# Keeping split weight parts in DRAM, lending idle PSUM banks and re-ordering a written-out instruction list in a one-core transformer layer

## The chip, the cores and the metric

The kernel runs on one core of a Trainium2 chip. The metric is the device time of one execution in microseconds (us). Five engines work side by side, each through its own instruction stream in order: TensorE (PE, matmuls), VectorE (DVE), ScalarE (ACT), GpSimd (POOL) and SyncE (SP, which here only issues DMAs). POOL also issues DMAs, through a queue of its own.

## The reference

One decoder layer on 1024 tokens of width 1024: a half-step SwiGLU FFN, a mixing stage of two attentions side by side, and a second half-step FFN. The change lies in the mixing stage:

```python
merged = jax.nn.sigmoid(gate_a) * (y_a @ w_o_a[l]) + jax.nn.sigmoid(gate_b) * (y_b @ w_o_b[l])
x = x + merged @ w_out[l]
```

`gate_a` and `gate_b` are columns of one projection of the normed input, `y_a` is a sparse attention over the 256 best keys of each token, `y_b` a stick-breaking attention. `w_o_a` and `w_o_b` are 512 x 1024, `w_out` is 1024 x 1024, all in float32.

## The kernel before, in words

**Matrix products.** Every float32 operand is split in a high part (rounded to the PE's float32r by an ACT copy) and a low part (the rest, a subtraction on POOL or DVE), and each product is three matmuls: high x high, high x low, low x high (`mm3`, L310 to L314). A weight that is read raw from DRAM so costs an ACT copy and a POOL subtraction (`split`, L293; in the mixing stage `weights`, L1107).

**The order of the program.** First FFN, then the mixing stage, then the second FFN. In the mixing stage the order on PE, DVE, ACT and POOL is written out by a planner that runs when the program is built. Each piece of work is a Python generator that yields what it needs next; `Weave.run` steps the one that can start first by a table of durations (`Weave.cost`, L113), with ranks as tie-breaks. What it emits is the order that the chip then follows; the order is fixed, the waits are semaphores. Outside the mixing stage the tile framework's own scheduler orders the instructions, and it orders the SP stream everywhere.

**PSUM.** In the mixing stage there are eight banks of 128 x 512 float32: two `fbank` (projections: `psf` for gates, `psuv`, `psob`, `psoa`), three `ubank` (`psdot`, `psz`, later the logits `psL`), two `vbank` (transposes) and one `wbank` (`psy`, `pso`). A gate projection (`fproj`, L1196, called in `fillers`, L1285) is 24 matmuls in one `fbank`; ACT reads it out (`gate_out`, L1226) into a ring of three small tiles `evr`, and POOL stores it in DRAM (`gd`).

**The end of the mixing stage.** `project` (L2199) multiplies by `w_o_b` for both token halves (`psob`, stored as `obd`) and by `w_o_a` for the first half (`psoa`, stored as `md`); sets `oa0`, `oa2`, `oa4`, `oa6` are 256 columns each, as high and low tiles of 512 KB in a ring of four (two sets). The other half's `y_a` is ready last. So `w_o_a` is read and split again for it: `woa0`, `woa2` in the planned part, `woa4`, `woa6` behind it. There (L2247 on) `psm` are 8 x 12 matmuls; a tile `gate` takes `gd` and `obd` (two loads of 256 KB each), DVE multiplies and adds, and the result `m` is split (`M0`).

**w_out.** A second `project` (L2281) multiplies by `w_out` for one half, then for the other. Each half takes eight sets of `w_out` (`wout{half}{n}{j}`, 512 KB raw), 24 matmuls `psout` each. Raw tiles come from a ring of four, split parts from `op`, a ring of nine. The set for the second half is the same weight as for the first, read and split again. `x2d` stores the new residual; `b0r`, `b1r` are raw weights of the second FFN.

**A shared port.** The planner's table holds that POOL and DVE instructions with long operands in SBUF slow each other (`shared` in `flush`).

## Time and profile before

| | us |
|---|---|
| median of three runs (lowest, highest) | 2126.56 (2125.76, 2130.45) |
| the profiled execution | 2126.26 |
| its span, from the first to the last instruction | 2124.5 |
| PE busy in the span | 2100.6 |
| POOL, ACT, DVE busy | 913.5, 1063.6, 1521.6 |

A row of the timeline gives the start, the duration, the engine, the source line, the operation with its output and inputs, and in square brackets the idle time in front of it with what ended it. Matmuls are pipelined, so a matmul's duration is longer than the distance to the next one. A wait row gives who waited for whom: total us, how often, the longest. A row of windows gives, for a stretch of time, the busy time and count of each engine, the granted PE clock, the busy share of the 16 DMA engines and their GB/s.

### The profile page before, as it was taken

The numbers are of one execution on the slowest core, as the hardware profiler recorded it, in microseconds if no ns is written. First come the engines' busy times: TensorE is split into PE (matmuls) and PEld (weight loads), VectorE is DVE, ScalarE is ACT, GpSimd is POOL, SyncE is SP. The second block draws the span as 40 slices with busy tenths as digits, with TensorE's granted clock in tenths as the row PEclk, the third lists the DMA queues.
The fourth block names the chain that finished last, engine by engine and source line by source line (L and its number), as shares of the span: only waits on it lengthen the run. The fifth ranks groups of instructions, "written<-read, shape, count | busy, mean of one in ns | idle before, by whom it ended". The sixth has DMA issues, their size and how long they took to land.

```text
span 2124.5 us, 29820 instructions
## 1 busy us (share of the span) xinstructions
PE 2100.6 (99%) x10196; PEld 1762.4 (83%) x10196; DVE 1521.6 (72%) x2477; ACT 1063.6 (50%) x1998; POOL 913.5 (43%) x717
## 2 busy tenths in 40 slices
PE   8999999999999999999999999999999999999999
PEld 7888888888889988888887888778888888888887
DVE  7866767678875599788886588754755556488675
ACT  6343343334455356888886577535432322324443
POOL 6654555522345234322123342255665545542233
PEclk9999999999999999999999999999999999999999
DMA  5577877497685253686647755574143333259655
GB/s 150 160 245 219 251 203 237 151 328 249 212 231 167 76 159 105 224 217 165 171 157 231 258 165 169 190 257 151 50 129 100 104 95 129 95 185 330 222 175 188
DMA packets 298104, 387.79 MB, mean 183 GB/s; under 512 B 40144, under 2 KB 186224, under 8 KB 297952
## 3 DMA queue, kind: packets, MB, share of 16 engines
q1 hardware_dynamic: 285088, 343.90, 52.2%
q0 software_dynamic: 12864, 41.99, 5.5%
q8 instruction: 80, 1.31, 0.3%
q14 instruction: 72, 0.59, 0.1%
HBM read 264.67 MB, written 121.15 MB: 182 GB/s over the span
## 4 chain that ended last, share of the span: by engine, by line
PE 88%; issue 4%; DVE 3%; DMA 3%; POOL 1%; ACT 1%; SPq 0%; POOLq 0%; DVEq 0%; ACTq 0%
PE p L774 6%; PE p L775 6%; PE p L773 6%; PE pd L535 4%; PE pd L534 3%; PE pd L536 3%; PE pc L534 3%; PE pa L535 3%; PE pa L534 3%; PE pa L536 3%; PE pc L535 3%; PE pc L536 3%; PE psf L312 3%; PE psf L313 3%; PE psf L314 3%
## 5 line engine op out<-in xcount | busy, mean ns | idle before, releaser
L1374 ACT ACTIVATE junka<-u,cand,sig 128x1024 bf16<-128x1024 f32 (+3 forms) x124 | 134.5, 1085 | 5.0 <-DVE cand L1366 3.6
L1820 DVE TENSOR_TENSOR_SCAN left<-left,hidden 128x640 f32<-128x640 f32 (+3 forms) x64 | 88.9, 1409 | 2.0 <-ACT left L1814 1.8
L897 ACT ACTIVATE swh<-swr 128x512 fp32r<-128x512 f32 x48 | 30.2, 629 | 115.5 <-issue 52.5
L898 DVE TENSOR_TENSOR swr<-swr,swh 128x512 f32<-128x512 f32 x48 | 43.6, 908 | 37.8 <-ACT swh L897 37.6
L677 ACT ACTIVATE b0u<-b0u 128x512 f32<-128x512 f32 x20 | 12.6, 632 | 99.8 <-DVE b0u L557 84.4
L1874 DVE SCALAR_TENSOR_TENSOR pt<-pstT,pt 128x512 fp32r<-128x512 f32 (+1 forms) x96 | 51.4, 547 | 14.4 <-ACT pt L1871 13.8
L1871 ACT ACTIVATE pt<-pstT 128x512 fp32r<-128x512 f32 (+1 forms) x96 | 46.6, 495 | 16.6 <-PE pstT L1946 15.1
L1726 ACT ACTIVATE relu<-psdot 128x512 f32<-128x512 f32 (+1 forms) x80 | 40.7, 522 | 26.5 <-DVE u L1733 17.4
L1235 POOL DMA_DIRECT2D gd<-evg x32 | 18.0, 564 | 80.4 <-ACT evg L1230 59.4
L774 PE MATMUL p<-aT,aS 128*128 128x512 f32 x132 | 51.5, 390 | 1.0 <-DVE aT L387 1.0
L774 PE MATMUL p<-bT,bS 128*128 128x512 f32 x132 | 51.3, 389 | 0.0
L1733 DVE SCALAR_TENSOR_TENSOR u<-relu,WI,u 128x512 f32<-128x512 f32 (+1 forms) x70 | 49.2, 718 | 2.7 <-ACT relu L1726 1.7
L775 PE MATMUL p<-aT,aS 128*128 128x512 f32 x132 | 50.7, 389 | 0.0
L775 PE MATMUL p<-bT,bS 128*128 128x512 f32 x132 | 50.7, 389 | 0.0
L2000 ACT ACTIVATE e<-e,mx 128x768 f32<-128x768 f32 (+7 forms) x54 | 40.9, 759 | 13.3 <-DVE mx L1991 13.1
L773 PE MATMUL p<-bT,bS 128*128 128x512 f32 x132 | 47.0, 389 | 0.0
L1946 PE MATMUL pstT<-ident,left 128*128 128x128 f32 x288 | 45.8, 272 | 0.0
L773 PE MATMUL p<-aT,aS 128*128 128x512 f32 x132 | 44.9, 389 | 0.0
L1814 ACT ACTIVATE left<-psz 128x512 f32<-128x512 f32 (+2 forms) x96 | 43.4, 507 | 1.7 <-PE psz L1839 1.6
L1946 PEld LDWEIGHTS pstT<-ident,left 128*128 128x128 f32 x288 | 35.7, 140 | 8.2
L1370 DVE TENSOR_SCALAR_CACHE_REDUCE junkv<-u,cand 128x512 uint8<-128x512 f32 (+1 forms) x62 | 41.7, 673 | 0.8
L386 ACT ACTIVATE bT<-bt 128x512 fp32r<-128x512 f32 x44 | 26.2, 624 | 30.9 <-PE p L775 26.7
(3065 smaller groups left out, 8135.4 us busy)
## 6 DMA issues: line engine op xcount, KB each, us to landing
aw<-in_w_down_dram SPq DMA_DIRECT2D x33, 512.0 KB, 4.9
bw<-in_w_down_dram SPq DMA_DIRECT2D x33, 512.0 KB, 5.0
swr<-in_w_in_dram SPq DMA_DIRECT2D x48, 256.0 KB, 5.6
a0r<-in_w_gate_dram SPq DMA_DIRECT2D x22, 512.0 KB, 7.5
a1r<-in_w_up_dram SPq DMA_DIRECT2D x22, 512.0 KB, 7.2
b0r<-in_w_gate_dram SPq DMA_DIRECT2D x22, 512.0 KB, 4.1
b1r<-in_w_up_dram SPq DMA_DIRECT2D x22, 512.0 KB, 3.9
x<-in_x_dram SPq DMA_DIRECT2D x16, 512.0 KB, 6.2
```

Source lines behind the costliest of these rows:

```text
L312: nc.tensor.matmul(ps, ah, bh, start=first, stop=False)
L313: nc.tensor.matmul(ps, ah, bl, start=False, stop=False)
L314: nc.tensor.matmul(ps, al, bh, start=False, stop=last)
L534: nc.tensor.matmul(ps, a[:, c], b[k][:, HI], start=start and k == 0, stop=False, skip_group_check=True)
L535: nc.tensor.matmul(ps, a[:, c], b[k][:, LO], start=False, stop=False, skip_group_check=True)
L536: ins = nc.tensor.matmul(ps, a[:, l], b[k][:, HI], start=False, stop=k == 3, skip_group_check=True)
L773: nc.tensor.matmul(ps[q][m], S[:, h], T[:, HI], start=p == 0, stop=False)
L774: nc.tensor.matmul(ps[q][m], S[:, h], T[:, LO], start=False, stop=False)
L775: nc.tensor.matmul(ps[q][m], S[:, l], T[:, HI], start=False, stop=p == last)
L1374: nc.scalar.activation(junks[1][:, 0:(i + 1) * P], score[i], AF.Sign, scale=sig[:, b:b + 1], bias=cand.bitcast(F32)[:, b:b + 1], accum_out ...
L1820: nc.vector.tensor_tensor_scan(back, back, ones, 1.0, op0=ALU.mult, op1=ALU.max)
L1946: nc.tensor.transpose(tp[:, q * P:(q + 1) * P], A[n + q][:, j * P:(j + 1) * P], ident)
```

## The change

Five edits go together.

1. **Parts of `w_o_a` kept.** When PE begins a set `oa{d}` for the first half, a new stream stores its high and low tile to DRAM, by two DMAs that POOL issues. `woa0` and `woa2` are then loaded as parts, two loads of 512 KB each in place of one raw load, an ACT copy and a POOL subtraction. `woa4` and `woa6` too, now into tiles of the ring `r` that opens at that point and no longer into the ring of four.
2. **Parts of `w_out` kept.** In the first half each set's parts are stored by two POOL DMAs; the second half loads parts, two SP loads of 512 KB per set, with no raw tile, ACT copy or POOL subtraction.
3. **Idle banks.** Between the last `psz` and the fourth gate set from the end, gates and `psuv` may take a `ubank` where it is free earlier than an `fbank`.
4. **Quarters.** POOL's subtraction for the `oa` sets is four instructions of 256 columns in place of one of 1024, and the planner may put other POOL work between them.
5. **Scattered durations.** In the planner's table each duration on DVE, ACT and POOL is multiplied by a random factor between 0.97 and 1.03 with a fixed seed, which changes the written order where two pieces of work were close.

```diff
+        self.luck = random.Random(67)
...
                 cost, late = self.cost(i, eng, outs, ins)
+                cost *= self.luck.uniform(1 - 0.03, 1 + 0.03) if eng != PE else 1.0
...
-                yield POOL, raw, wh
-                nc.gpsimd.tensor_tensor(wl[:, 0:m], raw[:, 0:m], f32(wh[:, 0:m]), op=ALU.subtract)
+                step = 256 if nm[:2] == "oa" else m
+                for c in range(0, m, step):
+                    yield POOL, raw, wh
+                    c = slice(c, c + step)
+                    nc.gpsimd.tensor_tensor(wl[:, c], raw[:, c], f32(wh[:, c]), op=ALU.subtract)
...
+        def filling():
+
+            return [fbank, ubank] if "sparse" in weave.marks and "warm" not in weave.marks else [fbank]
+
+        def first_of(rings):
+            return min(rings, key=lambda r: weave.when((r,), PE))
...
-                    yield PE, fbank, late(3)
-                    ps, cols = yield from fproj(s.parts, half, lambda: late(3))
+                    rings = filling()
+                    yield PE, rings, late(3)
+                    ps, cols = yield from fproj(s.parts, half, lambda: late(3), rings)
...
+        def weights_out(nm, *parts):
+            for to, w in zip(split_of[nm], parts):
+                weave.held[w.tensor.name] += 1
+                yield POOL, w
+                put_low(to, f32(w))
+                give(w)
...
                 wh, wl = W.parts
+                if nm == "oa":
+                    spawn(weights_out(f"woa{d}", *W.parts))
...
-                wh, wl = first.pop(0) if first else wcols(w_o_a, d * P, 2 * P, 0, 4, f"woa{d}")
+                if first:
+                    wh, wl = first.pop(0)
+                else:
+                    wh, wl = (rpool.tile([P, 1024], F32R, tag="r", name=f"woa{d}{part}", bufs=NR) for part in "hl")
+                    for w, part in zip((wh, wl), split_of[f"woa{d}"]):
+                        nc.sync.dma_start(f32(w), part)
...
-                        Ws[j] = wcols(w_out, n * 512, 512, j, 2, f"wout{half}{n}{j}", rawt=raw, wt=op)
+                        kept = split_of[f"wout{n}{j}"]
+                        if half:
+                            Ws[j] = [op(f"wout1{n}{j}{x}") for x in "hl"]
+                            for w, d in zip(Ws[j], kept):
+                                nc.sync.dma_start(f32(w), d)
+                        else:
+                            Ws[j] = wcols(w_out, n * 512, 512, j, 2, f"wout0{n}{j}", rawt=raw, wt=op)
+                            for w, d in zip(Ws[j], kept):
+                                nc.gpsimd.dma_start(d, f32(w))
```

PE executes the same matmuls as before. Its order is the same up to the middle of the first projections of the mixing stage and again from the last quarter of the `w_out` product on; between these the order is another one.

On PE, the place where the planned part ends and the `psm` matmuls begin, before: the last `pso` matmuls (attention values of the last head) stand directly ahead of the first `psm` on `woa0`.

```order
L2125 MATMUL pspT<-ident,e 128x128 x2
L2102 MATMUL pso<-pt,vh 128x384 x2
L2102 MATMUL pso<-pt,vh 128x128 x2
L2102 MATMUL pso<-morep_12157,vh 128x256 x2
L312 MATMUL psm<-y_12153,woa0h 128x512
L313 MATMUL psm<-y_12153,woa0h 128x512
L314 MATMUL psm<-y_12153,woa0l 128x512
```

The same place on PE in the changed program, in two pieces: the last `pso`, and the first `psm`. Between them stand the last twelve `psoa` matmuls on `oa6`.

```order
L2119 MATMUL pso<-pt,vh 128x384 x2
L2119 MATMUL pso<-pt,vh 128x128 x2
L2119 MATMUL pso<-morep_12181,vh 128x256 x2
L316 MATMUL psoa<-y_11362,oa6h 128x512
L317 MATMUL psoa<-y_11362,oa6h 128x512
L318 MATMUL psoa<-y_11362,oa6l 128x512
```

```order
L316 MATMUL psoa<-y_11365,oa6h 128x512
L317 MATMUL psoa<-y_11365,oa6h 128x512
L318 MATMUL psoa<-y_11365,oa6l 128x512
L316 MATMUL psm<-y_12177,woa0h 128x512
L317 MATMUL psm<-y_12177,woa0h 128x512
```

So twelve matmuls that need nothing from the last head moved behind its `pso`, and `oa6` is now used up to the first `psm`. Then come 24 `psm` on `woa0`, 24 on `woa2`, four on `woa4`'s high part, 12 `psout` of `wout000`, and the rest of `woa4` and `woa6`.

On SP, around the loads for this place, before: `woa4` and `woa6` are loaded raw ahead of the gates, and the first raw `w_out` sets too.

```order
L297 DMA woa4r<-in_w_o_a_dram 128x4x256
L297 DMA woa6r<-in_w_o_a_dram 128x4x256
L297 DMA wout002r<-in_w_out_dram 128x2x512
L297 DMA wout006r<-in_w_out_dram 128x2x512
L2254 DMA gate<-gd 128x512
L2255 DMA gate<-obd 128x512
```

On SP in the changed program the parts of `woa2`, which go into the tiles of `oa6`, stand after three of the sixteen gate loads; the parts of `woa4` and `woa6` stand behind all sixteen.

```order
L2285 DMA gate<-gd 128x512
L2286 DMA gate<-obd 128x512
L2285 DMA gate<-gd 128x512
L1120 DMA woa2h<-woa2hd 128x1024
L1120 DMA woa2l<-woa2ld 128x1024
L2286 DMA gate<-obd 128x512
```

```order
L2285 DMA gate<-gd 128x512
L2286 DMA gate<-obd 128x512
L2281 DMA woa4h<-woa4hd 128x1024
L2281 DMA woa4l<-woa4ld 128x1024
L2281 DMA woa6h<-woa6hd 128x1024
L2281 DMA woa6l<-woa6ld 128x1024
L301 DMA wout002r<-in_w_out_dram 128x2x512
```

So thirteen gate loads are queued between `woa2` and `woa4`, all behind a load that cannot start before PE is done with `oa6`; `wout000r` and `wout004r` moved ahead, into the planned part.

More of the change, by code (lines that the diff above doesn't have):

```diff
@@ L3 @@
 from math import prod
+import random
 import concourse.bass as bass
@@ L824, in trunk @@
     columns.update((f"wqk{base}{pr}", base + pr * P) for pr in range(4) for base in (C_QB, C_KB))
-    split_of = {nm: [dram.tile([P, 1024], F32, name=f"{nm}{part}d") for part in "hl"] for nm in columns}
+    split_of = {nm: [dram.tile([P, 1024], F32, name=f"{nm}{part}d") for part in "hl"]
+                for nm in (*columns, *(f"woa{d}" for d in range(0, ND, 2)), *(f"wout{n}{j}" for n in range(2) for j in range(0, ND, 2)))}
     rows_of = w_in[0].rearrange("(k p) f -> p k f", p=P)
@@ L1194, in proj_v, with fproj @@
             mark(f"v{n}", *outs, vd)
-        def fproj(W, half, rank=lambda: None):
+        def filling():
+            return [fbank, ubank] if "sparse" in weave.marks and "warm" not in weave.marks else [fbank]
+        def first_of(rings):
+            return min(rings, key=lambda r: weave.when((r,), PE))
+        def fproj(W, half, rank=lambda: None, rings=None):
             wh, wl = W
             cols = slice(half * 512, half * 512 + 512)
-            ps = fbank("psf")
+            ps = first_of(rings or [fbank])("psf")
             for k in range(ND):
@@ L1275, in proj_uv @@
         def proj_uv(t):
-            yield PE, "uv", f"vt{t}", fbank, late(3)
-            ps, vt, (uvh, uvl) = fbank("psuv"), VT[t], UV
+            rings = filling()
+            yield PE, "uv", f"vt{t}", rings, late(3)
+            ps, vt, (uvh, uvl) = first_of(rings)("psuv"), VT[t], UV
             mm3(ps, vt[:, 0:P], vt[:, P:2 * P], uvh, uvl, True, True)
@@ L1313, in fillers @@
                     t = len(UVS)
-                    if gates.index(g) >= UV_FROM and t < NT and weave.when(("uv", f"vt{t}", fbank), PE) <= weave.free[PE]:
+                    if gates.index(g) >= UV_FROM and t < NT and weave.when(("uv", f"vt{t}", filling()), PE) <= weave.free[PE]:
                         yield from proj_uv(t)
```

1 line of the change is left out of this document (added).

## The prediction

> **What bounds the kernel now.** I read the page's busy times first, then what PE waits for, then the timeline of the longest waits, then windows and DMA rows of the stretch where the change moves loads.
>
> ```profile
> span 2124.5 us, 29820 instructions
> PE 2100.6 (99%) x10196; PEld 1762.4 (83%) x10196; DVE 1521.6 (72%) x2477; ACT 1063.6 (50%) x1998; POOL 913.5 (43%) x717
> ...
> PE 88%; issue 4%; DVE 3%; DMA 3%; POOL 1%; ACT 1%; SPq 0%; POOLq 0%; DVEq 0%; ACTq 0%
> ```
>
> PE is busy for 2100.6 of 2124.5 us and holds 88% of the chain that ends last. The change removes no matmul, so it can only move the 23.9 us in which PE idles, the time it loses to a lower clock, and small gaps between matmuls. The waits of PE, longest in total first:
>
> ```profile
> PE psL L2037 <- DVE mx L1991: 2.4, 2, 2.2
> PE psdot L1755 <- ACT relu L1726: 1.7, 4, 0.6
> PE psf L312 <- ACT evg L1230: 1.5, 2, 1.2
> PE psf L312 <- DVE evl L1243: 1.5, 1, 1.5
> PE psm L312 <- DVE yt L1893: 1.4, 1, 1.4
> PE psout L313 <- POOL wout000l L301: 1.3, 1, 1.3
> ```
>
> Five of these six lie where the edits are: logits (`psL`), gates (`psf`), and the end of the mixing stage (`psm`, `psout`). They are short, so I price each from its place. For the distance of two undisturbed matmuls, and for the DMA rates at the end of the mixing stage, the windows:
>
> ```profile
> 1340.00:1350.00 10.00, 7.79 (x45) 6.46 (x44) 9.83 (x20) 6.75 (x14) 2.66 (x3) 1.00 0.37 118
> 1370.00:1380.00 10.00, 10.00 (x39) 8.03 (x38) 3.26 (x5) 1.70 (x3) 1.18 (x1) 0.85 1.01 359
> 1374.00:1386.00 12.00, 11.93 (x53) 9.55 (x52) 8.61 (x9) 3.79 (x5) 5.53 (x2) 1.00 0.99 360
> 1400.00:1430.00 30.00, 30.00 (x134) 24.83 (x133) 10.50 (x14) 9.41 (x14) 11.42 (x5) 1.00 0.81 296
> ```
>
> 134 matmuls in 30 us are 0.224 us each.
>
> **The change part by part.**
>
> *Idle banks.* PE around the three gate waits:
>
> ```profile
> 1113.82 0.28 PE L1928 MATMUL psy<-pt,vv 128*128 128x128 f32 x1
> 1115.26 0.50 PE L312 MATMUL psf<-mhi,wg1h 128*128 128x512 f32 x1 [1.17 <-ACT evg L1230]
> 1115.60 0.40 PE L313 MATMUL psf<-mlo,wg1h 128*128 128x512 f32 x1
> 1121.29 0.39 PE L314 MATMUL psuv<-uvh,vt 128*128 128x512 f32 x1
> 1122.04 0.50 PE L312 MATMUL psf<-mhi,wg2h 128*128 128x512 f32 x1 [0.37 <-ACT evg L1230]
> 1127.39 0.39 PE L314 MATMUL psf<-mhi,wg2l 128*128 128x512 f32 x1
> 1129.25 0.50 PE L312 MATMUL psf<-mhi,wg2h 128*128 128x512 f32 x1 [1.47 <-DVE evl L1243]
> ```
>
> A new gate starts 1.44, 0.75 and 1.86 us after the matmul before it. Without a wait the distances would be about 0.07 (a 128-column matmul), 0.23 and 0.23, so 3.5 us are lost. Each restart also costs 0.11 (the second matmul follows after 0.34 at 1115.60); that makes 3.9 us. Both `fbank` were still waiting for ACT or DVE to read them, while the three `ubank` had no more `psz` to serve. With three more banks PE can run three more groups of 24 x 0.224 = 5.4 us ahead of the read-out. What is late next is ACT's read-out itself, which no longer reaches PE within that reserve. I take 3.9; if the cover fails, 0.
>
> *Quarters.* The wait at the logits:
>
> ```profile
> 1339.18 2.38 POOL L1126 TENSOR_TENSOR oa6l<-oa6r,oa6h 128x1024 fp32r<-128x1024 f32 x1 [5.83 <-ACT oa6h L1124]
> 1339.20 2.90 DVE L2087 TENSOR_TENSOR y<-yt,y 128x512 fp32r<-128x512 f32 x1
> 1340.15 0.39 PE L314 MATMUL psoa<-y,oa4l 128*128 128x512 f32 x1
> 1342.75 0.45 PE L2037 MATMUL psL<-kkh,qs 128*128 128x384 f32 x1 [2.21 <-DVE mx L1991]
> L2087 DVE TENSOR_TENSOR y<-yt,y x8: 681/688/2899, 1191.5 to 1370.0; 128x512 fp32r<-128x512 f32 x8
> ```
>
> POOL begins its 1024-wide subtraction at 1339.18, DVE a two-input operation at 1339.20. The latter takes 2.90 us where the median of its line is 0.688, and ends just after POOL does; the logits' read-out stands behind it on DVE, and PE starts its next `psL` 2.60 us after the matmul before: 2.4 lost. In quarters DVE can go between:
>
> ```profile
> 1256.60 1.28 POOL L2182 TENSOR_TENSOR o<-o,gate 128x512 f32<-128x512 f32 x1 [0.60 <-ACT o L2177]
> L301 POOL TENSOR_TENSOR wout000l<-wout000r,wout000h x1: 2526/2526/2526, 1390.9 to 1390.9; 128x1024 fp32r<-128x1024 f32 x1
> L299 ACT ACTIVATE wout100h<-wout100r x1: 1062/1062/1062, 1429.9 to 1429.9; 128x1024 fp32r<-128x1024 f32 x1
> 1331.48 0.56 POOL L2196 DMA_DIRECT2D md<-o  x1 [9.13 <-DVE o L2194]
> ```
>
> 512 columns take 1.28 and 1024 take 2.38, so 256 would take about 0.73 (an estimate from the two): DVE is held up by 0.7 at most, and POOL pays 4 x 0.73 - 2.38 = 0.5 us per set, 2 us over four sets. That is hidden: POOL is busy 43% of the span by the page. I take 2.4 gained; the bounds are 0 (another wide subtraction meets DVE in the new order) and 2.4.
>
> *The end of the mixing stage.* PE at the first `psm`, and at the first `wout000l`:
>
> ```profile
> 1367.07 0.85 PE L2102 MATMUL pso<-morep,vh 128*128 128x256 f32 x2
> 1369.32 0.53 PE L312 MATMUL psm<-y,woa0h 128*128 128x512 f32 x1 [1.41 <-DVE yt L1893]
> 1391.16 1.07 PE L312 MATMUL psout<-wout000h,m 128*128 128x512 f32 x4
> 1393.51 0.50 PE L313 MATMUL psout<-wout000l,m 128*128 128x512 f32 x1 [1.28 <-POOL wout000l L301]
> ```
>
> The `psm` wait of 1.41 us is the way from the last `pso` over ACT and DVE; it ends 2.25 after the start of the last pair. The twelve `psoa` that now stand there last 12 x 0.224 = 2.7 us, so it goes, with its 0.1 for the restart. The clock goes with it: the window from 1370 shows 0.85 and 39 matmuls where 44.7 would fit, 1.5 us lost (0.15 x 10). The `psout` wait of 1.28 plus 0.1 came since `wout000`'s tile was `woa4`'s before; now it is `woa0`'s, free 5.4 us after the first `psm`. ACT (1.06), a store's issue (0.56) and POOL (2.53) then end at about 9.6, and PE needs it after 52 `psm`, at 11.6. This cover is 2 us; should it fail, 1.3 comes back. Sum gained: 1.5 + 1.5 + 1.4 = 4.4.
>
> *What the same edits add there.* SP's issues in the trace, and what these loads weigh:
>
> ```profile
> 1367.94 0.37 SPq L297 DMA_DIRECT2D wout002r<-in_w_out_dram  x1
> 1368.36 0.46 SPq L297 DMA_DIRECT2D wout006r<-in_w_out_dram  x1
> 1368.87 0.46 SPq L2254 DMA_DIRECT2D gate<-gd  x1
> 1379.45 0.32 SPq L2255 DMA_DIRECT2D gate<-obd  x1
> gate<-gd SPq DMA_DIRECT2D x8, 256.0 KB, 5.6
> gate<-obd SPq DMA_DIRECT2D x8, 256.0 KB, 5.7
> wout002r<-in_w_out_dram SPq DMA_DIRECT2D x1, 512.0 KB, 3.6
> ```
>
> Before, two raw sets and sixteen gate loads (5.24 MB) were issued from 1367.94 to 1379.45 and the last landed some 5.7 us later: 17.2 us, the DMA engines full (share 0.99 to 1.01 at 359 to 360 GB/s in the windows). `woa4` was there already. Now SP stands at `woa2h` until PE has finished `oa6`, which is the first `psm`, and everything behind it stands too. Count from there: `woa2` is needed after 24 matmuls, 5.4 us, and lands at about 0.4 + 3.6 = 4.0 (the landing time of 512 KB in an idle stretch), so it is in time. `woa4h` comes behind 1.05 MB of `woa2` and 13 gate loads of 262 kB; with its own 0.52 MB that is 4.98 MB, and by the old burst's pace 17.2 x 4.98 / 5.24 = 16.3 us. PE wants it after 48 matmuls, at 10.8. So a new wait of 5.5 us, on a DMA. It covers what comes after: `woa4l`, `woa6`, `wout002r`, `wout006r` follow at 1.5 us each, by 24, while PE after its stall reaches `wout002` only at 32; ACT and POOL need 1.06 + 0.56 + 2.53 of these 8. Bounds: 0, if the gates flow faster or are early; 8.4, if the stores of `wout000`'s parts (1.05 MB from POOL's queue, 2.9 us at 360 GB/s) go in between. I take 5.5, nearest to the measured burst, and no loss of clock: the 2.2 us wait at 1342.75 left it at 1.00 (window from 1340), the 1.41 us wait did not. If it comes, it costs 1.5.
>
> The Trainium skill (DMA: Bandwidth & Descriptors, "Issuing engines are not separate DMA queues") says that transfers from SP and from POOL run on the same 16 DMA engines and interleave. By that rule the upper bound holds and the sum below would be smaller by 2.9; no row of before has wide stores in such a burst. The Trainium skill (TensorE: Matmul & The Clock Gate, "What's actually happening") has the clock halved after a window of about 3.4 us of idling, which a wait of 5.5 us would hold; by it the sum would be smaller by 1.5. The trace halved it after 1.41 us already, so the rule is not the whole of it here.
>
> *Work taken off ACT and POOL.* Twelve splits go: 12 x 1.06 = 13 us of ACT and 12 x 2.4 = 29 us of POOL, against 24 store issues of 0.56 = 13 us. None of it but `wout000l` was on PE's path, so it counts for nothing. The loads of `w_out`'s second half double to 1.05 MB per 5.4 us (195 GB/s), below the 296 of the window from 1400; the stores add as much there, which is the weak point below.
>
> *Scattered durations.* The order moves on all engines from the middle of the first projections to the `w_out` product. The small waits there (1.7 us behind `relu`, others of half a us) have as good a chance to grow as to shrink. I take 0, between -4 (they all go, with their restarts) and +5 (two waits like the 2.4 at the logits come).
>
> **The sum.** -3.9 - 2.4 - 4.4 + 5.5 + 0 = -5.2. The profiled execution took 2126.26 us, 1.8 more than its span and 0.3 below the median of 2126.56, so I add nothing for it: 2121.1.
>
> **The rivals.**
>
> *No new wait at `woa4`.* The gates may flow ahead of `woa2`'s turn or land faster. For it: 360 GB/s is a mean, three gate loads do stand ahead. Against: the SP order, in which thirteen stand behind. 2126.3 - 10.7 = 2115.6, about 2113 to 2118.
>
> *The scattered order gives the gain back.* New meetings of POOL and DVE, or banks late elsewhere, of 2.4 us each: two of them make 2125.9, between 2122.5 and 2129. For it: `ob` sets and values keep their wide subtractions. Against: PE waits are few in the whole stretch.
>
> *Slower: the stores fill the DMA engines.* In 45 us of the first `w_out` half 8.4 MB of stores come to the 296 GB/s of the window from 1400: 296 + 187 = 483, where 360 is all that the full windows show. Then `woa4h` waits 8.4, the clock loses 1.5, and the loads of the second half's first sets queue behind x rows, raw weights and stores: at 123 GB/s too much over 45 us, 5.5 MB or 15 us are late, of which the three sets of lead hide some 10. New waits 8.4 + 1.5 + 5 = 14.9 and a scattered order that costs 1 or more: 2131 or so. It decides from 10.7 + 4.3 = 15 us of new waits on. Against: SP's sets are issued early, and only one of them is needed per 5.4 us.
>
> That the edits don't take effect is no rival: the written order shows each.
>
> **How the numbers follow.** 0.2%, 4.3 us, is about what a measurement of this kernel can tell from no change; faster means below 2122.3. Forecast (2118 to 2124): 0.38, of which 0.27 lie below that bound and 0.11 within. No new wait: 0.22, faster. Scattered order: 0.24, of which 0.02 faster, 0.20 within, 0.02 slower. Slower: 0.16, of which 0.14 past the bound. That makes faster 0.51, same 0.33, slower 0.16. The range, 2113 to 2130, leaves out the lower end of the second case and the worse half of the last.
>
> **What would show it.** Right: no `psf` wait on `evg` or `evl` between the last `psz` and the first `psL`; no DVE operation of 2.9 us beside an `oa` subtraction; a `psm` that waits some 5 us for a DMA of `woa4h` right after 48 others; `psout` without a wait on `wout000l`. Wrong: a `woa4h` landed within 10 us of the first `psm`, new waits of `psL` or `psdot` above 4 us in sum, or `psout` waiting for `wout1` loads.

## The result, and the profile after

The changed kernel takes 2141.57 us (median of 4 runs, 2140.50 to 2142.49); beside it on the same chip the kernel before took 2127.17 (4 runs). The ratio is 1.0065, 95% interval 1.0048 to 1.0083: slower by 14.4 us, and above the range of the prediction. The page of the changed kernel:

```profile
span 2140.4 us, 29878 instructions
PE 2105.6 (98%) x10196; PEld 1769.6 (83%) x10196; DVE 1516.2 (71%) x2481; ACT 1049.7 (49%) x1982; POOL 896.5 (42%) x741
```

The span grew by 15.9 us, PE's busy time by 5.0 with the same 10196 matmuls. So about 11 us are new idle time, and the rest are matmuls that ran at a lower clock. What PE waits for now, longest first (who waits, for whom, total us, times, longest):

```profile
PE psm L316 <- DMA woa4h<-woa4hd: 8.6, 1, 8.6
PE psg L418 <- DMA bg<-in_g_ffn_dram: 6.4, 1, 6.4
PE psdot L1772 <- ACT relu L1743: 4.1, 4, 2.0
PE psout L316 <- DMA wout100l<-wout00ld: 1.9, 1, 1.9
PE psout L317 <- POOL wout014l L305: 1.4, 1, 1.4
```

The waits of gates (`psf`), of the logits on `mx`, of the first `psm` on `yt` and of `psout` on `wout000l` are gone, as foreseen. Four of the five rows are new, all around `w_o_a`'s and `w_out`'s loads; the `psdot` row has grown from 1.7 to 4.1. The stretches where they lie (columns as before: PE, PEld, DVE, ACT, POOL busy with counts, granted clock, DMA share, GB/s):

```profile
820.00:830.00 10.00, 7.29 (x31) 5.42 (x30) 9.97 (x14) 5.25 (x10) 5.36 (x5) 0.87 0.27 84
830.00:840.00 10.00, 10.00 (x60) 9.51 (x59) 6.04 (x17) 4.07 (x9) 2.05 (x4) 0.79 0.29 114
1375.00:1390.00 15.00, 6.42 (x21) 5.01 (x21) 3.67 (x5) 2.29 (x4) 1.10 (x2) 0.77 1.03 404
1440.00:1450.00 10.00, 1.94 (x9) 1.26 (x7) 3.37 (x9) 4.27 (x8) 1.14 (x2) 0.76 1.05 398
1450.00:1460.00 10.00, 9.74 (x37) 8.15 (x38) 2.04 (x7) 0.48 (x1) 1.10 (x2) 0.73 1.07 386
```

The same stretches in the kernel before:

```profile
820.00:830.00 10.00, 9.13 (x59) 7.88 (x58) 8.15 (x17) 6.70 (x14) 4.91 (x6) 1.00 0.39 131
1375.00:1390.00 15.00, 14.93 (x66) 12.05 (x65) 12.47 (x16) 5.30 (x8) 5.53 (x2) 1.00 0.82 300
1440.00:1450.00 10.00, 10.00 (x46) 8.29 (x45) 5.67 (x10) 4.78 (x8) 7.12 (x6) 1.00 0.69 238
```

In the changed kernel PE works from 1375 on 6.42 of 15 us, and from 1440 on 1.94 of 10, both times with the DMA engines full (share 1.03 to 1.05, 398 to 404 GB/s). In and behind each of the three stretches the granted clock is 0.73 to 0.87. From 1450 on PE is busy nearly all the time, yet does 37 matmuls in 10 us.

The first of these places in the timeline:

```profile
1364.14 0.32 SPq L1120 DMA_DIRECT2D woa2h<-woa2hd  x1
1374.33 0.32 SPq L2286 DMA_DIRECT2D gate<-obd  x1
1374.82 0.39 PE L318 MATMUL psm<-y,woa2l 128*128 128x512 f32 x1
1375.01 0.32 SPq L2281 DMA_DIRECT2D woa4h<-woa4hd  x1
1383.79 0.77 PE L316 MATMUL psm<-y,woa4h 128*128 128x512 f32 x1 [8.58 <-DMA woa4h<-woa4hd]
```

SP issues `woa4h` at 1375.01, behind the gate loads, which is when PE has finished with `woa2`; PE waits for all of its 8.7 us in flight. The second place:

```profile
1431.14 5.62 SPq L2309 DMA_DIRECT2D x<-xd  x4
1436.85 0.45 SPq L504 DMA_DIRECT2D b0r<-in_w_gate_dram  x1
1437.40 5.49 SPq L414 DMA_DIRECT2D bg<-in_g_ffn_dram  x1
1443.07 0.34 SPq L2335 DMA_DIRECT2D wout100h<-wout00hd  x1
1448.09 0.24 PE L418 MATMUL psg<-ident,bg 8*128 8x8 f32 x1 [6.38 <-DMA bg<-in_g_ffn_dram]
1450.26 2.05 PE L316 MATMUL psout<-wout100h,m 128*128 128x512 f32 x4 [1.93 <-DMA wout100l<-wout00ld]
```

The gain row of the second FFN (`bg`, 4 KB) stands on SP behind four `x` rows and raw FFN weights, and the first set of the second half, `wout100`, behind `bg`: it is issued at 1443.07, when PE has been idle for more than a microsecond. (In the kernel before, `wout100`'s raw set was issued at 1420.62.) The third place:

```profile
824.35 2.36 POOL L1134 TENSOR_TENSOR wvb11l<-wvb11r,wvb11h 128x1024 fp32r<-128x1024 f32 x1 [2.26 <-ACT wvb11h L1129]
824.35 2.90 DVE L1750 SCALAR_TENSOR_TENSOR u<-relu,WI,u 128x512 f32<-128x512 f32 x1
827.93 0.69 PE L1772 MATMUL psdot<-kih,qsi 128*128 128x384 f32 x1 [2.01 <-ACT relu L1743]
```

That is the case of `oa6l` again, at a set that was not cut in quarters: a 1024-wide subtraction on POOL, a DVE operation of 2.90 us that starts with it, and PE waits 2.01 us behind it. The Trainium skill (SBUF — State Buffer, "SBUF: two separate sides") has POOL and such a DVE operation share a port that the first one locks for its whole instruction; the two equal starts and the 2.90 agree with it.

**One measure for all runs.** To add up losses by place, idle and clock together, I take for each matmul the distance to the next one, less the median distance of matmuls of its width and type in the kernel before, and sum by stretches of the trace (us from the start of the span):

| run | to 800 | 800 to 850 | 850 to 1100 | 1100 to 1150 | 1150 to 1250 | 1250 to 1350 | 1350 to 1400 | 1400 to 1500 | sum |
|---|---|---|---|---|---|---|---|---|---|
| before | 11.3 | 2.2 | 3.2 | 4.6 | 0.8 | 5.7 | 6.1 | 0.0 | 34.6 |
| after | 12.5 | 8.5 | 2.5 | 0.5 | 0.8 | 2.1 | 10.5 | 12.4 | 50.6 |
| `out_again` | 11.1 | 8.4 | 2.5 | 0.6 | 0.9 | 2.1 | 8.9 | 0.0 | 35.4 |
| `stores_only` | 11.1 | 5.8 | 2.8 | 0.6 | 1.3 | 2.0 | 10.7 | 8.7 | 43.9 |
| `bg_early` | 12.8 | 7.3 | 2.6 | 0.8 | 0.9 | 2.0 | 11.1 | 13.2 | 51.4 |
| `oa_again` | 12.4 | 7.2 | 2.7 | 0.5 | 1.0 | 2.1 | 0.6 | 17.0 | 44.3 |
| `no_scatter` | 11.6 | 2.2 | 3.5 | 0.2 | 9.9 | 2.1 | 17.0 | 9.4 | 56.5 |
| `banks` | 11.3 | 2.1 | 4.2 | 0.2 | 10.3 | 2.8 | 2.9 | 0.0 | 34.7 |
| `banks_quarters` | 12.4 | 2.2 | 3.8 | 0.2 | 9.1 | 2.1 | 1.3 | 0.0 | 31.7 |
| `quarters` | 12.5 | 2.2 | 4.5 | 4.1 | 0.8 | 2.6 | 4.8 | 0.0 | 32.3 |
| `all_quarters` | 13.6 | 3.2 | 4.0 | 0.2 | 9.3 | 2.2 | 1.3 | 0.0 | 34.5 |
| `banks_quarters_scatter` | 12.3 | 8.4 | 2.6 | 0.8 | 0.9 | 2.0 | 0.6 | 0.9 | 28.5 |
| `bqs_wvb` | 15.2 | 3.9 | 4.3 | 0.3 | 6.0 | 1.2 | 0.0 | 0.0 | 31.7 |
| `out_woa_pool` | 13.5 | 8.2 | 2.7 | 0.9 | 0.8 | 2.1 | 9.3 | 0.0 | 38.2 |
| `woa46_raw` | 10.9 | 7.3 | 3.3 | 0.9 | 1.3 | 2.1 | 0.6 | 0.9 | 27.2 |
| `half_gates` | 11.9 | 7.3 | 3.0 | 0.5 | 0.9 | 2.0 | 4.3 | 0.7 | 30.6 |

(The sum has the stretch past 1500 too, from -0.1 to 0.8. The first column holds the start of the program, where PE waits for the first loads, and differs by up to 4 us. Each row is one execution, the profiled one, which lies up to 3 us from the median of its run: the table shows where a loss lies, the times and ratios below show how much a change is worth.) Before against after: -4.1 at the gates, -3.6 at the logits; +6.3 from 800 to 850, +4.4 from 1350 to 1400, +12.4 from 1400 to 1500; +1.2 in the first column.

### The profile page after: what moved, and what is told of

The parts are those of the page before. It is cut to its first block, busy times and chain, and to the rows that moved or that the text cites. A ratio compares the mean times of both kernels' runs of the same rounds, so it can differ in the third digit from the quotient of the medians.

```text
span 2140.4 us, 29878 instructions
## 1 busy us (share of the span) xinstructions
PE 2105.6 (98%) x10196; PEld 1769.6 (83%) x10196; DVE 1516.2 (71%) x2481; ACT 1049.7 (49%) x1982; POOL 896.5 (42%) x741
## 4 chain that ended last, share of the span: by engine, by line
PE 89%; DVE 5%; DMA 3%; ACT 1%; issue 1%; SPq 0%; POOL 0%; DVEq 0%; ACTq 0%; POOLq 0%
PE p L778 6%; PE p L779 6%; PE p L777 6%; PE psf L316 4%; PE psf L318 3%; PE pd L538 3%; PE pd L540 3%; PE psf L317 3%; PE pd L539 3%; PE pc L538 3%; PE pa L538 3%; PE pa L540 3%; PE pa L539 3%; PE pc L540 3%; PE pc L539 3%; PE pb L540 2%
## 5 line engine op out<-in xcount | busy, mean ns | idle before, releaser
L1391 ACT ACTIVATE junka<-u,cand,sig 128x896 bf16<-128x896 f32 (+3 forms) x124 | 134.2, 1082 | 3.1 <-DVE cand L1383 1.6
L1891 DVE SCALAR_TENSOR_TENSOR pt<-pstT,pt 128x512 fp32r<-128x512 f32 (+1 forms) x96 | 51.3, 547 | 15.5 <-ACT pt L1888 14.6
L390 ACT ACTIVATE bT<-bt 128x512 fp32r<-128x512 f32 x44 | 26.0, 623 | 30.6 <-PE p L779 26.5
```

What stands on the lines that cost most here:

```text
L1391: nc.scalar.activation(junks[1][:, 0:(i + 1) * P], score[i], AF.Sign, scale=sig[:, b:b + 1], bias=cand.bitcast(F32)[:, b:b + 1], accum_out ...
```

## The experiments

Each kernel was compared with the kernel before on the same chip. The edits have the numbers of the change: 1 parts of `w_o_a`, 2 parts of `w_out`, 3 idle banks, 4 quarters, 5 scattered durations. Most expectations set a theory against a rival; the text behind each says which of them the run bears out.

| run | what it is | us | before beside it | ratio (95%) |
|---|---|---|---|---|
| `out_again` | all but 2 | 2127.32 | 2128.58 | 0.9992 (0.9983 to 1.0002) |
| `oa_again` | all but 1 | 2137.05 | 2128.58 | 1.0042 (1.0028 to 1.0057) |
| `no_scatter` | all but 5 | 2149.37 | 2128.58 | 1.0099 (1.0084 to 1.0114) |
| `banks_quarters` | 3, 4 | 2126.50 | 2128.58 | 0.9998 (0.9988 to 1.0007) |
| `stores_only` | all, stored parts of `w_out` not read | 2136.72 | 2128.06 | 1.0040 (1.0025 to 1.0055) |
| `bg_early` | all, `bg` loaded ahead | 2142.95 | 2128.06 | 1.0066 (1.0049 to 1.0083) |
| `banks` | 3 | 2127.12 | 2128.06 | 0.9998 (0.9988 to 1.0007) |
| `all_quarters` | 3, 5, quarters for every set | 2128.33 | 2128.06 | 1.0001 (0.9992 to 1.0010) |
| `banks_quarters_scatter` | 3, 4, 5 | 2119.47 | 2127.87 | 0.9956 (0.9941 to 0.9971) |
| `bqs_wvb` | 3, 4, 5, quarters for `wvb` too | 2122.03 | 2127.87 | 0.9970 (0.9958 to 0.9982) |
| `out_woa_pool` | all but 2, `woa4`, `woa6` from POOL | 2127.88 | 2127.87 | 1.0000 (0.9990 to 1.0009) |
| `quarters` | 4 | 2124.84 | 2127.87 | 0.9983 (0.9974 to 0.9993) |
| `woa46_raw` | all but 2, `woa4`, `woa6` raw | 2119.37 | 2129.12 | 0.9960 (0.9948 to 0.9973) |
| `half_gates` | all but 2, half the gate loads | 2121.90 | 2129.12 | 0.9971 (0.9959 to 0.9983) |

### One edit undone at a time

The parts of `w_out` undone (`out_again`):

```diff
-                        kept = split_of[f"wout{n}{j}"]
-                        if half:
...
-                        else:
...
+                        Ws[j] = wcols(w_out, n * 512, 512, j, 2, f"wout{half}{n}{j}", rawt=raw, wt=op)
```

> The changed kernel without the kept parts of w_out: each half loads the raw weights and splits them itself, as in the kernel before; all else as changed. Theory (the DMA traffic of these stores and doubled loads makes bg, wout100h and wout014l late): the waits of 6.4, 1.9 and 1.4 us at 1429 to 1450 and the clock's loss behind them (about 4) go, so some 11 to 13 us less than the changed kernel's 2141.6: 2128 to 2131. The woa4h wait of 8.6 at the end of mixing gets shorter at most by the 2.9 us that the stores of wout000 were priced at. Rival (it is only that bg stands behind x rows and FFN weights on SP's queue): bg's wait stays above 4 us, and the time stays above 2136.

2127.32, by ratios 15.5 us less than the changed kernel (0.0073 of 2128): the theory has the direction and the place, but more goes than its 11 to 13 us, and the time lies just below its range. Of the new waits only the one on `woa4h` is left, and from 1440 on the engines are no longer full:

```profile
PE psm L316 <- DMA woa4h<-woa4hd: 5.9, 1, 5.9
```

```profile
1440.00:1450.00 10.00, 10.00 (x46) 8.28 (x45) 5.50 (x9) 5.57 (x9) 7.31 (x6) 1.00 0.45 149
```

PE is busy throughout at full clock, with a DMA share of 0.45 where the changed kernel has 1.05. Edit 2 is what turns the change from no difference into a loss.

The parts of `w_o_a` undone (`oa_again`):

```diff
-                if nm == "oa":
-                    spawn(weights_out(f"woa{d}", *W.parts))
...
-                if first:
-                    wh, wl = first.pop(0)
-                else:
...
+                wh, wl = first.pop(0) if first else wcols(w_o_a, d * P, 2 * P, 0, 4, f"woa{d}")
```

> The changed kernel without the kept parts of w_o_a: they are split again at the end of mixing, as in the kernel before; all else as changed. Theory: the woa4h wait (8.6) and the clock's loss behind it (about 3.4) go, the three small losses of the kernel before there (4.4 in sum: 1.41 psm wait, 1.28 wout000l wait, clock) come back, so 2141.6 - 12.0 + 4.4 = 2134. Rival (the w_out traffic alone fills the engines there): a wait of 5 us or more for a DMA stays in the stretch 1365 to 1400, and the time stays above 2138.

2137.05. The `woa4h` wait goes and nothing else takes its place at 1350 to 1400 (0.6 in the table), so the rival is out; but the three small losses of the kernel before did not come back there either, and the time is above the 2134 of the theory. What came instead is more loss in the `w_out` stretch, 17.0 for 12.4: the burst of stores now meets `wout014h` and `wout102h` (waits of 4.0 and 1.7) beside `bg` (5.8). The two kept sets disturb each other's timing, so their costs do not simply add.

The list planned without scatter (`no_scatter`):

```diff
-                cost *= self.luck.uniform(1 - 0.03, 1 + 0.03) if eng != PE else 1.0
```

> The changed kernel with the list planned from unscattered durations; all else as changed. In its list SP issues all gate loads ahead of woa2h, and woa4 and woa6 come right behind woa2. Theory (the scattered order put 13 gate loads between woa2 and woa4, and a wide POOL subtraction beside a DVE operation in the second projections): the woa4h wait with its clock loss (12.0) and the psdot waits with theirs (about 6) both go, and bg's wait stays or moves to the loads behind it: 2141.6 - 18 = 2123.5. Rival (the scattered order costs only the psdot waits; woa4h is late by traffic and its slot): the woa4h wait stays above 4 us, time 2133 to 2136. Third: the order is neutral, 2140 to 2143.

All three expectations miss: 2149.37, slower still. The `psdot` loss goes (2.2 from 800 to 850), as the theory has it, but two others come:

```profile
PE psm L315 <- DMA woa0h<-woa0hd: 7.5, 1, 7.5
PE psm L315 <- DMA woa2h<-woa2hd: 4.2, 1, 4.2
PE pspT L2141 <- DVE e L2028: 2.8, 1, 2.8
```

With the gate loads ahead of the parts, it is `woa0h` and `woa2h` that are late and not `woa4h`. And the stretch from 1150 to 1250 loses 9.9, with a `pspT` wait that neither kernel has. So the scattered order is worth some 7 us to the changed kernel (0.0034 of 2128); the theory, which had it only cost, falls.

Idle banks and quarters alone (`banks_quarters`: edits 1, 2 and 5 taken out as above).

> The kernel before with the idle banks and the quarters alone. Both theories: the psf waits on evg and evl (3.9 with restarts) and the psL wait (2.4) go, nothing else moves: 2127.2 - 6.3 = 2120.9. If the quarters give part of it back on POOL, or the new order makes other waits, 2123 to 2127.

2126.50, ratio 0.9998: no difference, in the second range of the expectation. The waits named are gone or small (the one on `mx` is 0.6), and the same `pspT` wait of 2.7 is there. The scatter or the kept parts must keep it away in the changed kernel.

### Idle banks and the written order

The idle banks alone (`banks`), that is `banks_quarters` with

```diff
-                step = 256 if nm[:2] == "oa" else m
+                step = m
```

> The kernel before with the idle banks alone. With banks and quarters together the waits of gates and logits and those at the end of mixing went, but a wait of 2.7 us on pspT and others of 5 us in sum came between 1200 and 1250. Theory (gates that run earlier in idle banks are spent when the softmax of the logits starts, and PE has nothing to put beside it): pspT and pso waits of 5 us or more in that stretch, time 2127 to 2130 with the psL wait of 2.4 still there. Rival (the quarters re-ordered the list there): no such waits, 2122 to 2124.

2127.12, no difference again, and the wait is there without the quarters: the idle banks bring it. The `psL` wait of 2.4, which the theory had kept, is 0.6 here without any quarters: the new order alone took it away. The waits of `banks`, and the stretch:

```profile
PE pspT L2141 <- DVE e L2028: 3.3, 3, 2.8
```

```profile
1200.00:1250.00 50.00, 44.23 (x230) 36.49 (x229) 32.12 (x88) 31.94 (x74) 17.21 (x16) 0.97 0.72 243
```

PE is busy 44.23 of 50 us (50.00 in the kernel before). The list of PE shows why. Here, in the list of `banks`, from the last gate to the first `psob`:

```
L317 MATMUL psf<-mhi_5640,wg7l 128x512
L2118 MATMUL pso<-pt,vh 128x512 x2
L2118 MATMUL pso<-pt,vh 128x384 x2
L2118 MATMUL pso<-pt,vh 128x128 x2
L2118 MATMUL pso<-pt,vh 128x256 x2
L2141 MATMUL pspT<-ident,e 128x128 x10
...
L2141 MATMUL pspT<-ident,e 128x128 x10
L315 MATMUL psob<-yb_12192,ob0h 128x512
```

44 matmuls of the softmax chain, each group waiting for ACT and DVE, with nothing independent between. In the kernel before, in the changed one, and in `quarters`, `out_again` and `banks_quarters_scatter` six matmuls (`psL`) stand there. The theory said that the gates are spent earlier; they aren't (the last `psf` starts at 1203.7 before, at 1202.1 in `banks_quarters`). It is the mixture: gates that ran ahead are missing between the groups, and `psob` begins late. Over the lists the count goes with the loss: 16 matmuls there (`all_quarters`) or 44 (`banks`, `banks_quarters`, `no_scatter`), 9.1 to 10.3 us from 1150 to 1250; six, 0.8 to 1.3, but for `bqs_wvb` below, whose loss there has another place. No run changed this place alone, so that the chain is the cause is read from the lists, not shown. Why the planner writes it so isn't settled; small differences of its durations tip it.

Edits 3, 4 and 5 (`banks_quarters_scatter`: the kept parts taken out, the rest as changed).

> Edits 3, 4 and 5 without any kept parts. In its list 7 matmuls stand from the last gate to the first psob, as in the kernel before; where 17 or 45 stand there (banks, banks_quarters, no_scatter, all_quarters) the stretch 1200 to 1250 lost 8 to 10 us. Theory (that place in the list decides, and the scattered order is worth what it saves there; edits 1 and 2 are what made the whole change slower): no loss at 1200, psdot waits with their clock of 6.3 as in the changed kernel, gate and logits waits gone: 2128 - 7 = 2121, 2119 to 2123. Rival (the scattered order costs as much elsewhere as it saves): 2125 to 2128.

2119.47, ratio 0.9956: faster than both kernels. The stretch from 1200 on, and the one where `psm` stands:

```profile
1200.00:1250.00 50.00, 49.89 (x277) 43.18 (x277) 37.21 (x106) 36.62 (x89) 20.58 (x20) 1.00 0.77 244
1375.00:1390.00 15.00, 14.79 (x65) 11.92 (x65) 13.50 (x15) 6.30 (x8) 7.74 (x3) 1.00 0.49 166
```

49.89 of 50 us busy, and 14.79 of 15 at full clock without any kept part. In its list the last `psoa` stand behind the last `pso` too: that move, and so the gain at the end of mixing, belongs to the list and not to the parts of `w_o_a`.

### The subtraction and the shared port

The quarters alone (`quarters`).

> The kernel before with the quarters alone; 7 matmuls from the last gate to the first psob. Theory (the term of 2.4 us of the prediction holds): the psL wait behind DVE goes, nothing else moves, 2125 to 2126. Rival (the wait comes back at another meeting of POOL and DVE): 2127 to 2129.

2124.84, ratio 0.9983 (0.9974 to 0.9993), 3.6 us: theory. From 1250 to 1350 it loses 2.6 for 5.7, and no DVE operation from 1335 to 1345 lasts over 1.5 us.

Quarters for all sets, without kept parts (`all_quarters`):

```diff
-                step = 256 if nm[:2] == "oa" else m
+                step = 256
```

> Idle banks, scattered durations, and the subtraction in quarters for all weight sets, not for those of w_o_a alone; no parts of w_o_a or w_out are kept. Theory (the psdot wait of 2.0 us, the one of 1.6 and the clock behind them, 6.3 in sum against before, come from a 1024-wide POOL subtraction beside a two-input DVE operation of 2.9 us): these go, so do the gate and logits waits, and nothing is added at the end of mixing: 2127.5 - 3.9 - 2.4 - 4 = 2117, between 2114 and 2120. Rival (the psdot waits come from the order, whatever the width): psdot waits of 3 us or more stay, 2121 to 2125.

2128.33: the total misses, since its list has 16 matmuls between the last gate and the first `psob` and loses 9.3 us from 1150 to 1250. The `psdot` loss, on which the two differ, did shrink: 3.2 from 800 to 850 instead of the 8.4 of `banks_quarters_scatter`. To have the one without the other, quarters for `oa` and `wvb` alone, in a list with six (`bqs_wvb`):

```diff
-                step = 256 if nm[:2] == "oa" else m
+                step = 256 if nm[:2] == "oa" or nm[:3] == "wvb" else m
```

> As banks_quarters_scatter, with POOL's subtraction in quarters for the two sets wvb10 and wvb11 too; 7 matmuls from the last gate to the first psob here as well. Theory (a 1024-wide POOL subtraction of wvb holds DVE for 2.9 us and makes the psdot waits of 2.0 and 1.6 with the clock's loss of 6.8 us at half speed): 5 to 6 us below banks_quarters_scatter, 2115 to 2117. Rival (the psdot waits are the order's, whatever the width): the same as banks_quarters_scatter within 1.5.

2122.03, not better than without (2119.47), and above both ranges. The port is cleared: beside the four subtractions of `wvb11l` no DVE operation lasts over 1.21 us, and 800 to 850 loses 3.9 for 8.4. But the new list has a new meeting:

```profile
826.12 3.72 POOL L1134 TENSOR_TENSOR wvb11l<-wvb11r,wvb11h 128x256 fp32r<-128x256 f32 x4 [1.46 <-ACT wvb11h L1129]
1162.19 2.29 DVE L1444 TENSOR_TENSOR_SCAN cum<-eq 128x1024 f16<-128x1024 f16 x1
1167.81 0.39 PE L2054 MATMUL psL<-kkh,qs 128*128 128x256 f32 x1 [2.85 <-DVE mx L2008]
```

The four quarters take 3.72 us for 2.36 (the row gives all four), and at 1167.81 PE waits 2.85 us for a row maximum that stands on DVE behind a scan of 2.29. From 1150 to 1250 it loses 6.0 for 0.9. So the wide subtraction had its part in the loss at 800, and a local gain is lost to the new order. The order has its part too: with the same wide subtraction the kernels without scatter (before, `quarters`, `banks`) lose 2.1 to 2.2 there, since in their lists the DVE operation that meets it lasts only 1.86 to 1.88 us.

### What makes w_out's parts expensive

The stores alone (`stores_only`):

```diff
-                        if half:
...
-                        else:
-                            Ws[j] = wcols(w_out, n * 512, 512, j, 2, f"wout0{n}{j}", rawt=raw, wt=op)
+                        Ws[j] = wcols(w_out, n * 512, 512, j, 2, f"wout{half}{n}{j}", rawt=raw, wt=op)
+                        if not half:
                             for w, d in zip(Ws[j], kept):
                                 nc.gpsimd.dma_start(d, f32(w))
```

> The changed kernel with the stores of w_out's parts in the first half, but the second half loads and splits the raw weights again, so the stored parts are not read. Only the stores (8.4 MB from POOL's queue, 1380 to 1430) are added to the run without edit 2, which took 2127.3. Theory S (the stores fill the DMA engines and make everything behind them late): a wait of bg or of a wout1 set of 4 us or more comes, 2136 to 2142. Rival F (the second half's use of parts is what costs: its loads are doubled to 1.05 MB per set, and the raw tiles that it leaves free let SP issue weights of the second FFN ahead of bg and wout100): no such wait, 2126 to 2130.

2136.72: in the range of theory S, though not by one long wait. By ratios the stores cost 10.2 us of the 15.5, the reading of the parts the other 5.3.

```profile
PE psm L316 <- DMA woa4h<-woa4hd: 8.3, 1, 8.3
PE psout L316 <- ACT braw L473: 2.0, 1, 2.0
PE psg L418 <- DMA bg<-in_g_ffn_dram: 1.7, 1, 1.7
PE psout L317 <- POOL wout014l L305: 1.5, 1, 1.5
```

```profile
1440.00:1450.00 10.00, 8.32 (x34) 6.57 (x34) 2.30 (x8) 6.11 (x10) 5.03 (x4) 0.83 0.99 369
```

From 1400 to 1500 there are three waits of 1.5 to 2.0, the clock is down to 0.83, and the engines are nearly as full as in the changed kernel (0.99). `woa4h` waits 8.3 for 5.9: the stores of `wout000` reach back into that burst. The landing of the `x` rows, loads that no edit touches, in `stores_only` and then in `out_again` (issued from 1375 to 1450):

```profile
x<-xd SPq DMA_DIRECT2D x8, 512.0 KB, 10.7
x<-xd SPq DMA_DIRECT2D x8, 512.0 KB, 6.1
```

The stores do two more things: they take 0.5 to 0.6 us of POOL each, and they hold their tiles of the ring `op` until they have landed. No run parts these from the bytes; but from 1365 to 1475 no engine's wait in `stores_only` or in the changed kernel names the landing of such a store, so the late loads are the likelier cause.

The gain row out of the way (`bg_early`; `bgrow` is a tile of its own, loaded ahead of the `psm` part):

```diff
+            bgrow = cst.tile([P, P], F32, name="bgrow")[0:ND, :]
+            nc.sync.dma_start(bgrow, g_ffn2[0].rearrange("(k p) -> k p", p=P))
...
-            R.gain()
+            R.gain(rows=bgrow)
```

> The changed kernel with the 4-KB gain row of the second FFN (bg) loaded into a tile of its own far ahead, and not from its place on SP's queue behind x rows and FFN weights. Theory (the DMA engines are full there, so the loads that stand next to bg are as late): the wait of 6.4 us moves from bg to wout100h, which landed at 1450.2 where bg landed at 1447.8; it starts one place earlier, so at most 1 to 2 us go: 2139 to 2142. Rival (only the place and the slot of bg in the queue): the 6.4 us and about half of the clock's loss of 4 go, 2131 to 2134.

2142.95, no gain. The wait moves to the first matmul on `wout100h`, as the theory has it (the row names another load, `wout102h`), and is longer:

```profile
1450.86 2.04 PE L316 MATMUL psout<-wout100h,m 128*128 128x512 f32 x4 [9.17 <-DMA wout102h<-wout02hd]
```

PE goes on at 1450.86, where it did so at 1450.26 in the changed kernel. So the place of this one load on the queue is not the cause. SP now stands for 5.53 us at `wout100h` (issued at 1438.04), as it stood for 5.49 at `bg`; what holds it there the profile doesn't show. But 512 KB issued around that time are 7.1 (`wout100h`) to 12.0 us in flight. The longest landing in the changed kernel among those issued from 1430 to 1446:

```profile
b0r<-in_w_gate_dram SPq DMA_DIRECT2D x1, 512.0 KB, 12.0
```

### What makes woa4h late

The four loads on POOL's queue (`out_woa_pool`, without the parts of `w_out`):

```diff
-                        nc.sync.dma_start(f32(w), part)
+                        nc.gpsimd.dma_start(f32(w), part)
```

> The changed kernel without the kept parts of w_out (2127.3) and with the four loads of woa4 and woa6 issued by POOL and not by SP, so that they do not stand behind 13 gate loads on one queue; the same bytes move. Theory (the place on SP's queue makes woa4h late): the woa4h wait falls from 5.9 to 2.5 or less and the clock's loss behind it goes: 2119 to 2122. Rival (the traffic there, gates and parts together, makes it late whatever the queue): a wait of 4.5 or more for woa4 stays or goes over to a gate, 2125 to 2129.

2127.88, with a wait of 5.1 us at the same place: no gain, the rival's range.

```profile
1374.09 0.55 POOL L2281 DMA_DIRECT2D woa4h<-woa4hd  x1 [6.17 <-DMA gate<-gd]
```

POOL stood idle for 6.17 us and issued `woa4h` at 1374.09; in `out_again`, the same kernel but for the queue, SP issued it at 1373.90. It was 7.1 us in flight (5.9 from SP), landed at 1381.2, and PE went on at 1381.63 after 5.15 us. The Trainium skill (DMA: Bandwidth & Descriptors, "Issuing engines are not separate DMA queues") has the DMAs of all issuers run on the same 16 engines; that the load from POOL's queue was in flight for no less time than the one from SP's agrees with it.

What does POOL wait for, with no gate load ahead of it on its queue? The row names a gate load as the last, but the DMA waits for several things at once, the stores of the mixing stage among them. The last store of `md` was issued at 1367.37 and landed at 1373.38, 0.7 us ahead of the issue of `woa4h`. `woa4` goes into a ring that opens behind the planned part, in memory that the mixing stage's tiles held, so its first load also waits for that store to land. On SP's queue it is the other way round. The last wait of SP in `out_again`, the issue, and the last store of `md`, which was issued at 1364.92 and so landed at 1371.3:

```profile
SPq L2281 <- DMA gate<-gd: 0.2, 1, 0.2
1373.90 0.32 SPq L2281 DMA_DIRECT2D woa4h<-woa4hd  x1
md<-o POOLq DMA_DIRECT2D x1, 256.0 KB, 6.4
```

There the store had landed 2.6 us earlier, and the gate loads held SP. So two things hold the load, one close behind the other, and to take away the first alone brings nothing.

In the kernel before, the raw `woa4` goes into a ring that is there already, and only ACT and POOL write new tiles. Two more kernels look at the two holds. `woa4` and `woa6` raw again, the other parts kept (`woa46_raw`):

```diff
-                if first:
-                    wh, wl = first.pop(0)
-                else:
...
+                wh, wl = first.pop(0) if first else wcols(w_o_a, d * P, 2 * P, 0, 4, f"woa{d}")
```

> The changed kernel without the kept parts of w_out (2127.3), and with woa4 and woa6 read raw and split again as in the kernel before; woa0 and woa2 are still loaded as parts, with all four stores. Theory (woa4h is late because its new tile is free only after the mixing stage's last stores, some 8 us into the burst of gate loads; a raw tile is free before): no wait of 3 us or more between 1365 and 1395 and no loss of clock there, so the 8.3 us by which that stretch is above the run of edits 3, 4 and 5 go: 2118 to 2121. Rival (the parts' stores and loads of woa0 and woa2 crowd the burst): a wait of 3 us or more stays, 2123 to 2127.

2119.37: theory. The raw tiles are free early, and SP issued the two loads at 1329.11 and 1347.16, ahead of the gate loads. All four sets are still stored and two are still loaded as parts, and the stretch is as good as without any:

```profile
1375.00:1390.00 15.00, 14.78 (x66) 11.87 (x65) 13.95 (x14) 5.91 (x8) 7.94 (x3) 1.00 0.70 236
```

And with eight of the sixteen gate loads left out (`half_gates`; the products take no `obd`):

```diff
-                    nc.sync.dma_start(g[:, 512:1024], obd[r, 512:1024])
...
-                    nc.vector.tensor_add(m, m, g[:, 512:1024])
+                    nc.vector.tensor_add(m, m, m)
```

> The changed kernel without the kept parts of w_out (2127.3), with the eight loads of obd into the gate tiles left out; DVE adds the product to itself in place of obd, so the output is another one. 5 gate loads instead of 13 stand between woa2 and woa4, and 2.1 MB less are moved. Theory (the tile of woa4 is bound by the mixing stage's last stores): woa4h is issued no earlier than 1370.5, with a wait of 1.5 to 4 us left. Rival (the 13 gate loads and their bytes bind it): it is issued by 1368 and the wait is gone, below 1 us, 2118 to 2121.

The wait of SP, the store it waits for, and the issue:

```profile
SPq L2281 <- DMA md<-o: 5.8, 1, 5.8
```

```profile
md<-o POOLq DMA_DIRECT2D x1, 256.0 KB, 7.1
```

```profile
1372.34 0.32 SPq L2281 DMA_DIRECT2D woa4h<-woa4hd  x1
```

2121.90. SP has only five gate loads ahead and stands idle for 5.8 us on the last store of `md`, which was issued at 1364.76 and took 7.1 us to land. `woa4h` goes out at 1372.34, lands in 3.7 us, and PE waits 2.3. Theory on all counts: the tile alone would hold the load. But of the 5.9 us of `out_again` only 2.3 are left, and by ratios 4.5 us went (0.9992 to 0.9971) of the 6.8 that went in `woa46_raw`. So the gate loads, by their place and their bytes, have the larger part, and the tile the smaller one.

In the changed kernel the last `md` store was issued at 1366.10 and landed 6.6 us later, at 1372.7, which is 8.5 after the first `psm`. SP was still at the gate loads; it issued `woa4h` at 1375.01, and the landing took 8.7 us instead of 3.7.

## Why the prediction was wrong

The forecast summed small gains of PE's waits and one new wait. Step by step:

- **Idle banks, -3.9.** Right in place and size: 1100 to 1150 lost 4.6 before and 0.5 after. Not seen was that by itself the edit changes the list from 1150 on and loses 10 us there (`banks`). That the changed kernel keeps the gain is due to the scatter.
- **Quarters, -2.4.** Right: 3.6 by itself, with an interval that holds 2.4. The same meeting came up at `wvb11l`, a set that the edit leaves wide; the step on the scattered order allowed for that (two waits, +5) but counted 0.
- **End of mixing, -4.4.** The `yt` and `wout000l` waits went, as priced. They went because of the order of the list: `banks_quarters_scatter` has the same gain (0.6 lost for 6.1) with no part kept. To book it to the parts gave edit 1 a gain that it does not have; edit 1, added to 3, 4 and 5, costs 7.7 (0.9956 to 0.9992).
- **woa4h, +5.5.** The wait came at the place named, after 48 `psm`. Without the stores of `w_out` it is 5.9 (`out_again`), so the working by gate loads and bytes had the right size, and the trace agrees with it: there SP's last wait was for a gate load. With the stores it is 8.6 (8.3 in `stores_only`); that is the upper bound of 8.4, which the step named and did not take. What it did not see is the second hold, the tile, which alone leaves 2.3 (`half_gates`) and makes another queue useless (`out_woa_pool`). "No loss of clock" was wrong as well: 0.77 from 1375 to 1390, and the stretch loses some 2 us beyond the wait.
- **Parts of w_out, 0.** This is the step that failed and decides: "it counts for nothing" became +15.5, by ratios 10.2 for the stores and 5.3 for the reading of the parts. The rival "the stores fill the DMA engines" had the mechanism and the place, 483 GB/s wanted where 360 flow, `psout` behind late loads. Its price for late loads, 5, rested on three sets of lead. There was no lead: SP issued `wout100h` at 1443.07, after PE had run out of work, and the sign named for being wrong, a `psout` that waits for a `wout1` load, is in the profile (1.9). That a load that is needed seldom has time only holds if it is issued early, and with full engines everything ahead on SP's queue is late too.
- **Scattered durations, 0, between -4 and +5.** Against before it shows as the 6.3 from 800 to 850 (6.2 from `banks_quarters` to `banks_quarters_scatter`), past the upper bound; "as good a chance to grow as to shrink" took no side where the list in fact put a wide subtraction beside a DVE operation. The other thing that it does can't be seen against before at all: without it, edits 3 and 4 lose 8.2 us more from 1150 to 1250 (`banks_quarters` against `banks_quarters_scatter`). The step priced the edit as if it stood alone.

By the table, what was forecast and what came: gates -3.9 and -4.1, logits -2.4 and -3.6, end of mixing -4.4 + 5.5 and +4.4, the scattered order 0 and +6.3, the `w_out` stretch 0 and +12.4, with 1.2 more ahead of 800. The gains came; the failure lies in the transfers. Part of the agreement is luck: in `banks` the logits' wait goes without any quarters, and the gain at the end of mixing and the quiet stretch from 1150 to 1250 belong to the one written order that the scatter made, which the prediction had priced at 0.

By the ratios: -9.4 for edits 3, 4 and 5, +7.7 for edit 1, +15.5 for edit 2, 13.8 in all, as the ratio 1.0065 has it. How edits 1 and 2 share the cost depends on the order in which they are taken (`oa_again`: +18.3 for edit 2 first, then +4.9).

## What to carry to other kernels

A load that replaces computing must be priced at the moment when its tile is free and at the share of the DMA engines that the stretch has left, not at its landing time in an idle one; here 15.5 us came with the stores and loads of `w_out`'s parts, and 7.7 with loads that fell into a burst of others, since their tiles were not free ahead of it. Where a list is written by a planner, read the new list for stretches in which one dependent chain stands alone: six or 44 matmuls between two fillers went with a loss of 9 us here, more than any edit was meant to bring. And test edits apart: three of the five together are 8.4 us faster than the kernel before, and all five 14.4 slower.

## What the runs showed of the hardware

- The clock does not follow the length of a wait alone. In the changed kernel it fell to 0.87 and 0.79 around waits of 2.01 us and less. At the `pspT` matmuls near 1211 the same wait of 2.75 us brought 3.4 us at half clock in `banks` and in `no_scatter`, and none in `banks_quarters` (1.00 from 1200 to 1250). Around the waits of 6.4 and 8.6 it fell both times, to 0.73 to 0.77. In the clock records of these runs a stretch at half clock behind a wait lasts 3.4, 6.8 or 10.2 us. The Trainium skill (TensorE: Matmul & The Clock Gate, "What's actually happening") has a window of about 3.4 us that runs freely; that one wait is caught and another of the same length isn't would fit such a window, but no run here varied the phase.
- Cutting a 1024-wide POOL subtraction in four cost about what was estimated (0.5) where nothing met it: 2.81 to 2.84 us for three of the four `oa` sets of the changed kernel, for 2.38 to 2.41 in the kernel before. Beside busy DVE work it cost 0.9 to 1.4 (3.27 for `oa6l`, 3.72 for `wvb11l`), and was still the cheaper way where DVE was waiting.
- Landing times in full engines: 512 KB took 7.1 to 12.0 us in the changed kernel (issued from 1430 to 1446) where `woa4h` in `half_gates` took 3.7, and the last `md` store, 256 KB, took 6.0 to 7.1 us in the four runs named above.
